# Where the streamed operands of the split matmuls begin in SBUF: 224 bytes behind a multiple of 256

## Chip, cores and metric

The kernel runs on one core of a Trainium2 chip. The metric is the device time of one execution in microseconds; the time before is the median of three runs.

## What is computed

One encoder layer on x of 512 tokens x 1024 features, in float32: a half-step SwiGLU network, a mixer, a second half-step SwiGLU network and a last RMSNorm. In short (the reference, cut):

```
def swiglu(x, w1, w3, w2):
    return (jax.nn.silu(x @ w1) * (x @ w3)) @ w2

def hybrid_mixer(h, w_in, ...):
    proj = h @ w_in                      # A: 24 heads q,k,v; B: 8 query, 2 key/value heads; 2 gates
    o_a = dilated_attention(...)         # 3 groups of 8 heads, joined by their softmax denominators
    o_b = gqa_axial_attention(...)
    gates = jax.nn.sigmoid((pg + b_gate).reshape(B, S, N_BRANCHES, D))
    merged = gates[:, :, 0] * (o_a @ w_branch_a) + gates[:, :, 1] * (o_b @ w_branch_b)
    return merged @ w_out

    x = x + 0.5 * swiglu(rmsnorm(x, ffn1_norm[l]), ...)
    x = x + hybrid_mixer(rmsnorm(x, mix_norm[l]), ...)
    x = x + 0.5 * swiglu(rmsnorm(x, ffn2_norm[l]), ...)
```

The networks are 1024 x 2816 (w1, w3) and 2816 x 1024 (w2).

## The kernel before

Everything is held transposed: 128 features on the partitions, the 512 tokens along the free axis, 4 bytes an element. x is eight tiles of 128 x 512.

**Split matmuls.** A float32 operand is split into H, a rounded copy in the format fp32r (made by ACT, line 217 for weights), and L, the rest (made by DVE, line 218). `mm3` (lines 230 to 234) then makes one product of three matmuls: weights H by streamed H (line 232), the same weights H by streamed L (233), weights L by streamed H (234). Each of the three is a load of 128 x 128 weights and a stream of 256 or 512 columns. The load for a matmul runs beside the stream of the one before it.

**Weight tiles.** All weights come in tiles of 128 x 1024 from HBM, in the fixed order of `self.order`. `prep` (lines 201 to 220) splits the next one as soon as a buffer of the rings is free. The split goes to the ring `wh` (three pairs of buffers in the pool `wb`), and every fourth tile (number 3 modulo 4 in the order), where the stage has a pool `wx`, goes to `whx`, one pair more. A tile serves 24 matmuls of 512 columns: eight blocks of 128 x 128, three matmuls each. In a Strassen step it also serves 24, of 256 columns.

**Strassen.** Part of the networks' first products (`strassen`, `right`) and most of the projection of q and k are done in Strassen's form with seven instead of eight steps for two feature blocks. The steps A11, A12, S3 and S4 stream halves of h, the normed input (`hH`, `hL`); S1, A22 and S2 stream sums of such halves: `TH`, `TL` in the networks, `TQH`, `TQL` in the projection, where S3 takes its operand from there too. The first network does nine pairs of feature blocks in stretches of 2, 4 and 3, the projection five pairs, the second network ten in stretches of 3, 4 and 3. Between the stretches of a network come the products with w2 that stream `gg`, the activated products (line 446 writes them).

**The other products.** In the mixer `feat` streams h by 512 columns; `token` streams weights against h, for v and for branch B's projections; the branch and output products stream `oH`, `qH` and `mH` (with their L parts); branch B's attention streams `kH` and the flipped probabilities `PTH`.

PE's instructions are in an order written out by hand. The other engines take theirs from the order of the program.

**Where tiles begin.** A pool is laid out when it is opened, tags in the order in which they first appear, each buffer at a multiple of 32 bytes. Pools on the left grow upwards: the constants, then `wb`, then `tmp`, then those of the stage. Pools on the right (`side="right"`) grow downwards: h at the very top, then `bt` with `rel_bias`, then the pool of T. All streamed tiles have sizes that are multiples of 256, so what is behind a pool keeps its start modulo 256 unless a small tile comes between. From the order and the sizes follows where each begins, modulo 256:

| tile | begins at |
|---|---|
| hH, hL | 224 |
| TH, TL in the first network (below `rel_bias` of 96 bytes) | 128 |
| TH, TL in the second network | 224 |
| TQH, TQL; gg; qH, qL, kH, kL, vH, vL; oH, oL; mH, mL; PTH, PTL | 32 |
| weights in the ring wh | 160 |
| weights in the ring whx | 32 |

In the program the small tiles are these: `ms` (line 384) has 16 bytes in each of four buffers, so 32 bytes apart; `nm` and `lq` in branch B's attention (lines 963 and 966) 4 bytes in each of four; `F` (line 824) 64 bytes in each of two.

Of the kernel before, what the change touches and what calls it, by code (L numbers as in the profile page):

```python
# [11 lines left out]
F32 = mybir.dt.float32  # L12
# [41 lines left out]
def tile_at(li):  # L54
    if li < 4:
        return 256 * li, (256 if li < 3 else 128), (0 if li < 3 else 64)
    return GP + 256 * (li - 4), 256, 256
# [8 lines left out]
def f32(t):  # L66
    return t.bitcast(F32)


class Layer:  # L70
    def __init__(self, ctx, tc, a):
        self.tc, self.nc, self.a = tc, tc.nc, a
        ctx.enter_context(tc.manual_schedule(engines={mybir.EngineType.PE}))
        pool = lambda n, **k: ctx.enter_context(tc.tile_pool(name=n, **k))
        self.dram = pool("dram", bufs=1, space=DRAM)
        self.cst = pool("cst", bufs=1)
        self.wb = pool("wb", bufs=1)
        self.tmp = pool("tmp", bufs=4)
        self.psm = pool("psm", bufs=4, space=PSUM)
        self.psa = pool("psa", bufs=4, space=PSUM)  # L80
        nc = self.nc
        c = self.cst
        self.x = [c.tile([128, T], F32, name=f"x{d}") for d in range(NK)]
        self.par = c.tile([128, 48], F32, name="par")
        nc.scalar.dma_start(self.par, a["par"])
        self.ident = c.tile([128, 128], F32, name="ident")
        self.ones = c.tile([128, 1], F32, name="ones")
        nc.vector.memset(self.ones, 1.0)
        self.mhalf = c.tile([128, 4], F32, name="mhalf")
        nc.vector.memset(self.mhalf, -0.5)  # L90
        nc.scalar.activation(self.ones, self.ones, AF.Copy)
        self.r = c.tile([128, 8], F32, name="r")
        self.R = c.tile([128, T], F32, name="R")
        nc.gpsimd.memset(self.R, 0.0)
        self.acc = c.tile([128, T], F32, name="acc")
        self.open_h()
        self.gate_d = self.dram.tile([16, 128, T], F32, name="gate_d")
        self.qk_d = self.dram.tile([2 * NSQ, 128, T], F32, name="qk_d")
        self.items = ([("v", 0), ("v", 1), ("sw", 0), ("v", 2)] + [("g", j) for j in range(2)]
                      + [("qk", f) for f in range(NSQ, 12)] + [("g", j) for j in range(2, 9)]  # L100
                      + [("b", g) for g in range(3)] + [("g", j) for j in range(9, 16)])
        span = {"v": ("wav", 4), "qk": ("waq", 2), "g": ("wg", 1), "b": ("wb", 4)}
        self.order = self.ffn_order("a")
        for kind, n in self.items:
            if kind == "sw":
                self.order += [("swq", at) for at in self.slots(range(0, NSQ, 2))]
                continue
            name, m = span[kind]
            self.order += [(name, m * n + i) for i in range(m)]
        self.order += [("wab", i) for i in range(12)] + [("wo", i) for i in range(8)]  # L110
        self.order += self.ffn_order("b")
        self.raws, self.tiles, self.used, self.wx, self.TQ = {}, [], 0, None, None
        self.cap = len(self.order)
        self.rings = {k: [] for k in BUFS}
        self.index = {it[:2]: n for n, it in enumerate(self.order)}
        self.kind = [self.home(it) for it in self.order]
        self.todo = sorted((n for n, t in enumerate(self.kind) if t != "ws"), key=self.turn_of)
# [263 lines left out]
    def rpow(self, dst, src, inv):  # L381
        nc = self.nc
        n = dst.shape[-1]
        ms = self.tmp.tile([128, 4], F32, tag="ms", name="ms")[:, :n]
        nc.vector.tensor_scalar(ms, src, inv, EPS, op0=ALU.mult, op1=ALU.add)
        nc.gpsimd.tensor_tensor(dst, ms, self.mhalf[:, :n], op=ALU.pow)

# [194 lines left out]

    def bias_open(self, bp):
        self.bp = bp
        self.rel = bp.tile([32, 24], F32, name="rel_bias")
        self.nc.sync.dma_start(self.rel, self.a["rel_bias"])
        self.zd = self.dram.tile([8, 128, NV], F32, name="zd")
        self.vd = self.dram.tile([8, NV], F32, name="vd")
# [163 lines left out]
    def scores_a(self, hp, res):  # L752
        nc, ap, qk = self.nc, self.ap, self.qk[hp]
# [11 lines left out]
        for pair in range(4):  # L765
            banks = [self.aux("S") for _ in range(2)]
            heads = []
            for h in range(2):
                hs, ps, mv = slice(64 * h, 64 * h + 64), banks[h], []
                for u in range(2):  # L770
                    li = 2 * pair + u
                    n, o = tile_at(li)[1], 256 * u
# [13 lines left out]
            for h in range(2):  # L786
                for u in range(2):
                    li = 2 * pair + u
                    off, n, w0 = tile_at(li)
# [4 lines left out]
            for h in range(2):  # L794
                for li in (2 * pair, 2 * pair + 1):
                    off, n, _ = tile_at(li)
# [24 lines left out]
        nc.vector.tensor_mul(L, E, SO[:, :, :, 2:4])  # L821
        nc.vector.tensor_add(MN, L[:, 0], L[:, 1])
        nc.vector.reciprocal(MN, MN)
        F = ap.tile([128, 8, 2], F32, tag="F", name="F", bufs=2)
        nc.vector.tensor_mul(F, E[:, 0], MN)
        res += [P, F]

    def values_a(self, hp, P, F):
        nc, ap, V = self.nc, self.ap, self.V
# [8 lines left out]
        def scale(stage):  # L838
            for h in range(2):
                for li in (2 * stage, 2 * stage + 1):  # L840
                    off, n, _ = tile_at(li)
                    sl = P[h][:, off:off + n]
                    nc.vector.tensor_scalar(sl, sl, F[:, li, h:h + 1], None, op0=ALU.mult)

# [109 lines left out]
    def attn_b(self, pp):  # L954
        nc = self.nc
        qH, qL, kH, kL, vH, vL = self.qH, self.qL, self.kH, self.kL, self.vH, self.vL
        P, po, pend = {}, {}, []

        def score(h, i):
            ps = self.aux("Sb")  # L960
            s = slice(128 * i, 128 * i + 128)
            self.mm3(ps, qH[:, h, s], qL[:, h, s], kH[:, h // 4, :], kL[:, h // 4, :], True, True)
            nm = pp.tile([128, 1], F32, tag="nm", name="nm", bufs=4)
            nc.vector.tensor_reduce(nm, ps, axis=mybir.AxisListType.X, op=ALU.max, negate=True)
            p = pp.tile([128, T], F32, tag="P", name="Pb", bufs=8 + LAG)
            lq = pp.tile([128, 1], F32, tag="lq", name="lq", bufs=4)
            nc.scalar.activation(p, ps, AF.Exp, bias=nm, scale=1.0, accum_out=lq)
            nc.vector.reciprocal(lq, lq)
            nc.vector.tensor_scalar(p, p, lq, None, op0=ALU.mult)
            P[h, i] = p  # L970

        def flip(h, k):
            pt = self.aux("Tb")
            for j in range(4):
                nc.tensor.transpose(pt[:, 128 * j:128 * j + 128], P[h, j][:, 128 * k:128 * k + 128], self.ident)  # L975
            H, L = self.split(pp, pt, [128, T], "PTH", "PTL")
            fs = slice(128 * (h // 4), 128 * (h // 4) + 128)
            pend.append((h, k, vH[:, k, fs], vL[:, k, fs], H, L, k == 0, k == 3))

        def value():  # L980
            h, k, *args = pend.pop(0)
            if k == 0:
                po[h] = self.bank()
            self.mm3(po[h], *args)
            if k == 3:
                nc.scalar.copy(qH[:, h, :], po[h])
                nc.vector.tensor_sub(qL[:, h, :], po[h], f32(qH)[:, h, :])

        for s in range(37 + LAG):
            if s < 32:  # L990
                score(s // 4, s % 4)
            t = s - 4 - LAG
            if 0 <= t < 32:
                flip(t // 4, t % 4)
            if pend and t > 0:
                value()
            yield GAP_B
        assert not pend
# [226 lines left out]
```

## Time and profile before

| | us |
|---|---|
| median of three runs (1282.14 to 1282.67) | 1282.46 |
| the profiled execution | 1282.78 |
| its span, first to last instruction | 1281.0 |
| PE busy | 1266.8 |
| DVE busy | 887.8 |
| ACT busy | 586.5 |
| POOL busy | 118.9 |

PE is busy in 99% of the span, at a mean granted clock of 0.998. The busy time of a matmul is longer than its share of the span, because matmuls overlap: a row gives 394 ns for one of 512 columns, while the next one starts some 230 ns after it. So durations of PE are taken here from stretches of known content and not from the mean of one instruction.

### The profile page before, as it was taken

How to read it: one execution, taken by the hardware profiler on the slowest of the kernel's cores; microseconds unless marked ns; L12 is line 12 of the kernel's file. 1: busy time of each engine (PE TensorE's matmuls, PEld its weight loads, DVE VectorE, ACT ScalarE, POOL GpSimd, SP SyncE). 2: the span in 40 equal slices, each digit the busy share in tenths (PEclk: the TensorE clock that was granted, in tenths of full speed). 3: DMA queues.
4: the chain of work that ended last, by engine and by line, in shares of the span. 5: the costliest groups of instructions: out<-in, count | busy, mean ns of one | idle time of the engine just before them, and what ended most of it. 6: DMA issues, size and time to landing. Idle time of an engine off the chain costs nothing.

```text
span 1281.0 us, 19956 instructions
## 1 busy us (share of the span) xinstructions
PE 1266.8 (99%) x8002; PEld 1122.1 (88%) x8002; DVE 887.8 (69%) x1339; ACT 586.5 (46%) x867; POOL 118.9 (9%) x124
## 2 busy tenths in 40 slices
PE   9999999999999999999999999999999999999997
PEld 7897999899889999877888878888889989988996
DVE  7784688467783885667557898655577747874775
ACT  8551355145463442635334465543465415532553
POOL 1111101000210212100001100000301000100001
PEclk9999999999999999999999999999999999999999
DMA  8865766241484846632232210345737636743222
GB/s 298 227 187 167 182 190 189 89 109 55 144 218 142 218 131 208 189 116 85 92 111 83 99 66 25 108 163 165 237 89 181 191 90 176 196 148 104 62 83 67
DMA packets 85549, 181.91 MB, mean 142 GB/s; under 512 B 12480, under 2 KB 19024, under 8 KB 85456
## 3 DMA queue, kind: packets, MB, share of 16 engines
q1 hardware_dynamic: 67904, 140.74, 32.6%
q0 software_dynamic: 16832, 39.34, 15.2%
q8 instruction: 63, 1.03, 0.3%
q10 hardware_dynamic: 720, 0.55, 0.1%
q14 instruction: 30, 0.25, 0.1%
HBM read 168.98 MB, written 15.29 MB: 144 GB/s over the span
## 4 chain that ended last, share of the span: by engine, by line
PE 93%; DVE 3%; issue 1%; DMA 1%; ACT 1%; POOL 0%; SPq 0%; POOLq 0%; DVEq 0%
PE mm L232 24%; PE mm L234 24%; PE mm L233 24%; PE Y L232 3%; PE Y L234 3%; PE Y L233 3%; PE X L232 2%; PE X L234 2%; PE X L233 2%; PE S L785 1%; PE mm L836 1%; PE Tb L975 1%; PE T L854 1%; PE Sb L233 0%; PE Sb L234 0%
## 5 line engine op out<-in xcount | busy, mean ns | idle before, releaser
L217 ACT CAST wh<-wr 128x1024 fp32r<-128x1024 f32 x142 | 148.8, 1049 | 224.8 <-PE mm L233 142.0
L218 DVE TENSOR_TENSOR wl<-wr,wh 128x1024 fp32r<-128x1024 f32 x142 | 173.3, 1221 | 56.9 <-ACT wh L217 56.2
L232 PE MATMUL mm<-hH,wh 128*128 128x256 f32 (+1 forms) x600 | 200.5, 334 | 0.4 <-ACT hH L368 0.3
L234 PE MATMUL mm<-hH,wl 128*128 128x256 f32 (+1 forms) x600 | 196.3, 327 | 1.0 <-DVE wl L218 1.0
L233 PE MATMUL mm<-hL,wh 128*128 128x256 f32 (+1 forms) x600 | 196.1, 327 | 0.3 <-DVE hL L369 0.3
L232 PE MATMUL mm<-gg,wh 128*128 128x512 f32 (+1 forms) x376 | 143.1, 380 | 0.0
L234 PE MATMUL mm<-gg,wl 128*128 128x512 f32 (+1 forms) x376 | 142.6, 379 | 0.0
L233 PE MATMUL mm<-gg,wh 128*128 128x512 f32 (+1 forms) x376 | 142.5, 379 | 0.0
L232 PEld LDWEIGHTS mm<-hH,wh 128*128 128x128 f32 x600 | 112.9, 188 | 14.8 <-issue 3.2
L234 PEld LDWEIGHTS mm<-hH,wl 128*128 128x128 f32 x600 | 112.7, 188 | 12.4 <-DVE wl L218 1.4
L233 PEld LDWEIGHTS mm<-hL,wh 128*128 128x128 f32 x600 | 112.8, 188 | 10.1 <-DVE hL L369 0.8
L217 ACT CAST wh<-wa 128x1024 fp32r<-128x1024 f32 x48 | 50.4, 1050 | 102.5 <-PE mm L233 49.6
L500 DVE TENSOR_TENSOR u<-mm,R 128x512 f32<-128x512 f32 (+1 forms) x52 | 33.8, 649 | 85.0 <-PE mm L234 84.7
L218 DVE TENSOR_TENSOR wl<-wt,wh 128x1024 fp32r<-128x1024 f32 x48 | 58.7, 1223 | 38.1 <-ACT wh L217 37.6
L234 PE MATMUL mm<-TH,wl 128*128 128x256 f32 x304 | 84.7, 279 | 0.0
L232 PE MATMUL mm<-TH,wh 128*128 128x256 f32 x304 | 84.6, 278 | 0.0
L233 PE MATMUL mm<-TL,wh 128*128 128x256 f32 x304 | 84.6, 278 | 0.0
L232 PEld LDWEIGHTS mm<-gg,wh 128*128 128x128 f32 x376 | 70.8, 188 | 15.3 <-PE mm L234 0.9
L234 PEld LDWEIGHTS mm<-gg,wl 128*128 128x128 f32 x376 | 70.8, 188 | 14.1
L233 PEld LDWEIGHTS mm<-gg,wh 128*128 128x128 f32 x376 | 70.9, 188 | 13.8
L217 ACT CAST wh<-ws 128x1024 fp32r<-128x1024 f32 x48 | 50.4, 1051 | 71.0 <-PE mm L233 52.3
L218 DVE TENSOR_TENSOR wl<-wa,wh 128x1024 fp32r<-128x1024 f32 x48 | 58.6, 1221 | 31.2 <-ACT wh L217 31.0
(233 smaller groups left out, 3171.3 us busy)
## 6 DMA issues: line engine op xcount, KB each, us to landing
wr<-in_w2a SPq DMA_DIRECT2D x22, 512.0 KB, 3.3
wr<-in_w2b SPq DMA_DIRECT2D x22, 512.0 KB, 3.5
wt<-in_w13b SPq DMA_DIRECT2D x20, 512.0 KB, 4.1
wa<-in_w13b SPq DMA_DIRECT2D x20, 512.0 KB, 3.5
wt<-in_w13b POOLq DMA_DIRECT2D x20, 512.0 KB, 6.1
wt<-in_w13a SPq DMA_DIRECT2D x18, 512.0 KB, 3.5
wt<-in_w13a POOLq DMA_DIRECT2D x18, 512.0 KB, 6.2
wa<-in_w13a SPq DMA_DIRECT2D x18, 512.0 KB, 3.4
```

Source lines behind the costliest of these rows:

```text
L217: self.nc.scalar.copy(H, raw)
L218: self.nc.vector.tensor_sub(L, raw, f32(H))
L232: mm(out, lH, rH, start=start, stop=False, skip_group_check=more)
L233: mm(out, lH, rL, start=False, stop=False, skip_group_check=more)
L234: mm(out, lL, rH, start=False, stop=stop, skip_group_check=more)
L500: nc.vector.tensor_mul(u, ps, R)
L785: nc.tensor.matmul(*args, start=True, stop=True)
L836: nc.tensor.matmul(oc, v, p, start=st, stop=sp)
L854: nc.tensor.transpose(ps[:, 128 * b:128 * b + 128], P[h][:, c0 + 128 * b:c0 + 128 * b + 128], self.ident)
L975: nc.tensor.transpose(pt[:, 128 * j:128 * j + 128], P[h, j][:, 128 * k:128 * k + 128], self.ident)
```

## The change

Tiles move, and nothing else. A tile `even` of 64 bytes that nothing uses becomes the first in the pool `tmp`. `ms` grows to 64 bytes a buffer, `nm` and `lq` too, `F` to 128 and `rel_bias` to 256; each is cut back to its old shape where it is used. So all behind `tmp` on the left moves up by 64 + 4 x 32 = 192 bytes, and its start of 32 becomes 224; the ring whx is among it. `PT` and the probabilities move by 128 more (160 becomes 224), the flipped probabilities by 256 more. On the right T of the first network moves from 128 to 224. h stays at 224, and the ring wh, which lies below `tmp`, at 160.

```diff
+        self.tmp.tile([128, 16], F32, tag="even", name="even", bufs=1)
...
-        ms = self.tmp.tile([128, 4], F32, tag="ms", name="ms")[:, :n]
+        ms = self.tmp.tile([128, 16], F32, tag="ms", name="ms")[:, :n]
...
-        self.rel = bp.tile([32, 24], F32, name="rel_bias")
+        self.rel = bp.tile([32, 64], F32, name="rel_bias")[:, :24]
...
-        F = ap.tile([128, 8, 2], F32, tag="F", name="F", bufs=2)
+        F = ap.tile([128, 16, 2], F32, tag="F", name="F", bufs=2)[:, :8]
...
-            nm = pp.tile([128, 1], F32, tag="nm", name="nm", bufs=4)
+            nm = pp.tile([128, 16], F32, tag="nm", name="nm", bufs=4)[:, :1]
...
-            lq = pp.tile([128, 1], F32, tag="lq", name="lq", bufs=4)
+            lq = pp.tile([128, 16], F32, tag="lq", name="lq", bufs=4)[:, :1]
```

## Rows read from the trace of the kernel before

**Rows 1.** The page: busy us, share, instructions by engine; the chain's shares.

```profile
PE 1266.8 (99%) x8002; PEld 1122.1 (88%) x8002; DVE 887.8 (69%) x1339; ACT 586.5 (46%) x867; POOL 118.9 (9%) x124
...
PE 93%; DVE 3%; issue 1%; DMA 1%; ACT 1%; POOL 0%; SPq 0%; POOLq 0%; DVEq 0%
```

**Rows 2.** Busy time by stretch, PE alone: the seven Strassen stretches.

```profile
core 0: us, PE busy (x), PEclk, DMA share, GB/s
53.44:92.58 39.14, 39.14 (x337) 1.00 0.68 176
139.36:218.12 78.76, 78.76 (x673) 1.00 0.72 187
262.54:321.69 59.15, 59.15 (x506) 1.00 0.29 84
402.08:501.48 99.40, 99.40 (x842) 1.00 0.60 175
954.99:1012.86 57.87, 57.87 (x505) 1.00 0.71 185
1057.28:1133.65 76.37, 76.37 (x674) 1.00 0.72 189
1178.07:1235.39 57.32, 57.32 (x505) 1.00 0.29 86
```

**Rows 3.** The same view: second network; steps on whx begin at 963.47, 974.78, 1062.93.

```profile
954.99:974.78 19.79, 19.79 (x169) 1.00 0.76 176
963.47:966.30 2.83, 2.83 (x26) 1.00 0.66 216
974.78:1012.86 38.08, 38.08 (x338) 1.00 0.69 190
1060.10:1062.93 2.83, 2.83 (x27) 1.00 0.51 185
1062.93:1133.65 70.72, 70.72 (x627) 1.00 0.74 193
```

**Rows 4.** The first network: T at 142.19 (whx), 145.07, 156.28; the others h.

```profile
142.19:145.07 2.88, 2.88 (x27) 1.00 0.56 190
145.07:147.91 2.84, 2.84 (x27) 1.00 0.55 185
153.56:156.28 2.72, 2.72 (x27) 1.00 1.03 162
156.28:159.11 2.83, 2.83 (x26) 1.00 1.07 164
```

**Rows 5.** The projection (TQ, TQ on whx, h) and the last g products.

```profile
404.91:407.76 2.85, 2.85 (x26) 1.00 0.88 295
407.76:410.63 2.87, 2.87 (x26) 1.00 0.72 210
410.63:413.45 2.82, 2.82 (x26) 1.00 1.07 213
1252.03:1257.73 5.70, 5.70 (x49) 1.00 0.00 0
1257.73:1260.61 2.88, 2.88 (x27) 1.00 0.00 0
```

**Rows 6.** Groups by line: casts of raw weight tiles, wr at 160, wt at 32.

```profile
L217 ACT CAST wh<-wr 128x1024 fp32r<-128x1024 f32 x142 | 148.8, 1049 | 224.8 <-PE mm L233 142.0 <-PE mm L234 32.2 <-issue 23.1
...
L217 ACT CAST wh<-wt 128x1024 fp32r<-128x1024 f32 x48 | 50.4, 1049 | 64.5 <-PE mm L233 38.8 <-PE Y L233 15.3 <-issue 6.1
```

**Rows 7.** Stretches of 512 columns: h; oH, qH, mH; g on whx; g.

```profile
36.96:53.44 16.48, 16.48 (x74) 1.00 0.92 247
820.10:931.64 111.54, 111.54 (x482) 1.00 0.61 191
1024.01:1029.46 5.45, 5.45 (x26) 1.00 0.25 90
1029.46:1046.20 16.74, 16.74 (x73) 1.00 0.30 96
```

## The prediction

> **What bounds the kernel now.** I read the busy times and the chain that ended last first [rows 1]. PE is busy for 1266.8 of 1281.0 us and carries 93% of the chain; DVE has 3% and DMA 1%. So the time is what PE's matmuls take one after another, and the rest runs beside them. The chain doesn't say why a matmul takes as long as it does. Their busy times do not help either, since they overlap; what counts is the distance from one start to the next. For that I took, in the view of busy time by stretch, stretches that begin and end with a weight tile. A weight tile of a Strassen step serves 24 matmuls of 256 columns, a tile of the other products 24 matmuls of 512. (The view counts a few matmuls too many, those that straddle an edge; I divide by the count from the code.) The granted clock is 1.00, the level of 2.4 GHz, in each of these stretches, so it explains no difference. Below, "start" is a tile's first byte modulo 256.
>
> The seven Strassen stretches stand in [rows 2]: 63 steps in the first feed-forward network, 177.05 us together, 35 in the projection of q and k, 99.40 us, and 70 in the second network, 191.56 us. That is 2.81, 2.84 and 2.74 us for the same 24 matmuls. At 256 cycles of 2.4 GHz a matmul they would take 2.56 us. The second network, where T begins at 224 like h, is the fastest.
>
> Single steps show that there are three lengths, and little between them [rows 3 to 5]:
> - 2.72 us (113.3 ns a matmul). Only steps whose streamed operand begins at 224 have it.
> - 2.83 us (117.8 ns). Steps with the same streamed operand at 224 have this too; 2.84 with T at 128, 2.85 with TQ at 32, both with weights at 160.
> - 2.88 us (119.8 ns). Steps where streamed operand and weights both begin at 32 (TQ, and the last g products), and T at 128 with weights at 32.
>
> Whether a step with streamed start 224 takes 2.72 or 2.83 us depends on what came before it [rows 3]. The second network begins at 2.83 us and stays there for seven steps. Then comes a step with a tile of the whx ring (weights at 32), and it and the 13 steps behind it, most with weights at 160, take 38.08 us, 2.72 each. After the g products a step takes 2.83 again (1060.10), the first whx step turns it, and that and 25 more take 70.72 us, 2.72 each. A whx step doesn't always turn it: the first one, at 963.47, took 2.83. In the first network a whx step with h turns it as well (153.56), and the next step with T at 128 undoes it (156.28) [rows 4]. In none of the seven stretches does a step with weights at 160 turn 2.83 into 2.72 by itself.
>
> **The change part by part.** No instruction is added or removed but the allocation of a tile that nothing writes or reads. Shapes stay, so ms, nm, lq, F and rel_bias are written and read as before, only at other bytes. Does a start matter to ACT, DVE or the loads? A cast of a weight tile at 160 takes 1049 ns and of one at 32 takes 1049 [rows 6]. I cost the shift on these engines at nothing; DVE is busy 69% of the span and ACT 46% [rows 1], so some tens of ns more on an instruction would stay beside PE. No wait is added. What is left is the streaming on PE.
>
> *Products of 512 columns, weights at 160.* With h at 224 three blocks took 16.48 us, 5.49 a block; the branch and output products, with their operands at 32, took 111.54 us for 20 blocks, 5.58, and two g blocks 16.74, 5.58 as well [rows 7]. The change puts these operands at 224. There are 30 g blocks with weights at 160 and these 20: 50 x 0.085 = 4.3 us less. The last g products, of 256 columns with weights at 160, go from 2.85 a block (5.70 for two) [rows 5] to 2.83: four blocks, 0.1 us less.
>
> *Products of 512 columns on the whx ring.* Eleven g blocks have weights and operand both at 32, and the first of a pair of g blocks takes 5.45 [rows 7]. They will both be at 224. No row shows 224 with 224. The bounds are 5.45, the shortest block of 512 columns, and 5.58: 0 to +1.4 us over eleven blocks. I take 0, since equal starts stay equal starts.
>
> *Strassen steps with weights at 160.* The operand is at 224 everywhere. Bounds 2.72 and 2.83, and which of them holds is the question of what turns a step. Today only the whx tiles at 32 turn it, and the change takes these away: they move to 224.
>
> *Strassen steps on the whx ring*: 15, 9 and 17 of the 63, 35 and 70. Operand and weights both at 224, which no row shows. The bounds are 2.72 (rows with the streamed start 224; no row of 24 such matmuls is shorter) and 2.88 (rows with equal starts). I take 2.88. The reason is that what is read at the same time are two streams, the operand of one matmul and the weights of the next, so their distance should matter and not one start alone: h at 224 gives 2.72 with weights 64 away as with weights 192 away, equal starts give 2.87 and 2.88 in two different products (TQ, and g) [rows 5]. The row nearest in that sense is the one with equal starts.
>
> And behind such a step? Steps of TQ at equal starts are followed by steps of h with weights at 160 that take 2.82 (410.63) [rows 5], never 2.72. So I let all steps with weights at 160 take 2.827, and those on whx 2.875.
>
> The sum by stretch, today's from [rows 2]: first network (11 x 2.827 + 3 x 2.875) = 39.72 for 39.14, (21, 7) 79.49 for 78.76, (16, 5) 59.61 for 59.15: +1.77. Projection (26, 9): 99.38 for 99.40: 0. Second network (16, 5) 59.61 for 57.87, (21, 7) 79.49 for 76.37, (16, 5) 59.61 for 57.32: +7.15. Together +8.9 us. Four stretches will follow g products at 224, and their steps ahead of the first whx step (1, 1, 2 and 2) may begin at 2.72: up to 6 x 0.107 = 0.6 us less, which I count in full, because the products ahead of them will have the very start that they have.
>
> Total: +8.9 - 0.6 - 4.3 - 0.1 = +3.9 us. The profiled execution took 1282.78 us around its span of 1281.0; the median shown is 1282.46. From the median: **1286.3 us**, 0.3% slower. The change speeds up nearly everything that streamed from 32 or 128, and pays by losing the tiles that put the second network into its fast lane.
>
> The Trainium skill speaks against any effect at all. In "TensorE: Matmul & The Clock Gate" (Step-by-step: what each phase is for) it gives PE two independent read ports, so that loading the next weights takes nothing from the running matmul; by it no start matters and the time stays at 1282.5. The steps of 2.72, 2.83 and 2.88 us at one clock do not agree with that [rows 3, 5].
>
> **The rivals.**
> - *The streamed start alone counts (the other side).* Then whx steps at 224 turn the lane as those at 32 did, and every stretch becomes like the second network's: 191.56 / 70 = 2.737 us a step. First network 63 x 2.737 = 172.4 for 177.05, projection 95.8 for 99.40, second network unchanged, and the same 4.4 us on the other products: -4.6 - 3.6 - 4.4 = -12.6, **1269.9 us**. For it: T at 128 and T at 224 differ with the same weights [rows 3, 4]. Against it: the turn comes from a change of the weights' start alone. It decides from about one step in five on: a step in the fast lane is 0.107 us shorter, so 36 of the 168 pay off the 3.9 us of the forecast.
> - *The equal starts cost nothing but turn nothing either.* All 168 steps at 2.827: 178.1, 98.9 and 197.9, so +1.05 - 0.45 + 6.3 = +6.9, less 0.6 and 4.4: +1.9, **1284.3 us**.
> - *Starts don't matter*, and the lanes come from something else, such as the order of products: **1282.5 us**. Against it: 5.58 and 5.49 us a block in long uniform stretches.
>
> **How the numbers follow.** Forecast 0.62, streamed start alone 0.15, equal starts free 0.13, no effect 0.10. The forecast's own bounds are the whx blocks (0 to +1.4), the six steps behind g products, should they be slow after all (+0.6), and some fifteen others in the fast lane (-1.6), so 1284.7 to 1288.3. The range takes in the two cases between and leaves out the fast one: 1282.0 to 1288.5. About 0.2%, 2.6 us, is what a measurement of this kernel can tell from no change. Slower by more (above 1285.0): most of the forecast's 0.62 and a little of the third case, 0.55. Within: the rest of the forecast, most of the third case and the fourth, 0.29. Faster: 0.16.
>
> **What would show it.** Right: in the profile after, steps on whx tiles at 2.87 to 2.88 us in all three parts, other steps at 2.83 behind them, no long run of 2.72; g, branch and output blocks with weights at 160 at 5.49; the second network's stretches at about 59.6, 79.5 and 59.6 us; casts and subtractions as they were. Wrong: stretches of 2.72 behind a whx step (first rival), whx steps at 2.83 (second), or blocks of 5.58 that stay (third). A wait of PE that is not there now would fit none of these cases, since PE's idle time is nearly nothing today.

## The result, and the profile after

| | before | after |
|---|---|---|
| median, us | 1282.51 | 1274.93 |
| the profiled execution, us | 1282.78 | 1274.42 |
| its span, us | 1281.0 | 1272.6 |

The ratio is 0.994, with a 95% interval of 0.9925 to 0.9955: 7.6 us less. The forecast was 1286.3, with a range from 1282.0 to 1288.5. It was wrong in size and in sign.

The page of the changed kernel: busy time by engine, then casts of those raw weight tiles that the change moves, wt, now at 224 (the rows that answer to [rows 1, 6]).

```profile
PE 1259.8 (99%) x8002; PEld 1119.1 (88%) x8002; DVE 888.7 (70%) x1339; ACT 587.2 (46%) x867; POOL 118.7 (9%) x124
...
L218 ACT CAST wh<-wt 128x1024 fp32r<-128x1024 f32 x48 | 50.4, 1050 | 63.4 <-PE mm L234 38.1 <-PE Y L234 15.3 <-issue 4.7
```

The other engines are as they were to within 1 us, and a cast of wt takes 1050 ns where it took 1049. PE has the same 8002 matmuls and 7.0 us less of busy time, of 8.4 us between the two spans. So, as the prediction assumed, nearly all of it is the pace of PE's matmuls. In the rows that follow the columns are those of [rows 2]: the stretch, its length, PE's busy time and instructions, granted clock, DMA share, GB/s. First the seven Strassen stretches after, which answer to [rows 2]:

```profile
52.90:92.11 39.21, 39.21 (x338) 1.00 0.69 175
138.41:215.78 77.37, 77.37 (x673) 1.00 0.73 190
259.64:317.66 58.02, 58.02 (x506) 1.00 0.28 85
397.68:494.53 96.85, 96.85 (x842) 1.00 0.64 180
945.46:1004.01 58.55, 58.55 (x506) 1.00 0.72 186
1047.87:1125.35 77.48, 77.48 (x674) 1.00 0.72 186
1169.21:1227.33 58.12, 58.12 (x506) 1.00 0.30 86
```

By part they are 174.60 us in the first network, 96.85 in the projection, 194.15 in the second network: 465.60 together, where the kernel before needs 177.05 + 99.40 + 191.56 = 468.01. The prediction had 178.8, 99.4 and 198.7, less 0.6.

Then steps in the second network (first stretch, then the first two steps of the second), and in the projection, one at a time or three together. Steps on whx begin at 953.94, 965.30 and 403.33:

```profile
953.94:956.82 2.88, 2.88 (x27) 1.00 0.67 218
956.82:965.30 8.48, 8.48 (x75) 1.00 0.78 163
965.30:968.17 2.87, 2.87 (x27) 1.00 0.90 256
968.17:976.33 8.16, 8.16 (x75) 1.00 0.53 169
1047.87:1053.52 5.65, 5.65 (x50) 1.00 0.49 129
...
403.33:406.21 2.88, 2.88 (x27) 1.00 0.81 226
406.21:414.37 8.16, 8.16 (x75) 1.00 0.76 197
```

A whx step, operand and weights both at 224, takes 2.87 to 2.88 us. Behind the first one three steps take 8.48 us, 2.83 each. Behind the second three take 8.16, 2.72 each, and so does every step with weights at 160 from there to the end of the stretch. In the projection the first whx step, one of TQ, does it. Over the kernel 107 of the 127 steps with weights at 160 take 2.72 us and 20 take 2.82 to 2.83; all 41 whx steps take 2.87 to 2.88. The loads beside them don't set the pace: three short steps take 8.16 us at a DMA share of 0.53 and at one of 0.76.

Last, products of 512 columns, which answer to [rows 7]: the 20 blocks of the branch and output products, a g block on whx, the three g blocks behind it, and two of the last g blocks of 256 columns [rows 5].

```profile
812.24:922.12 109.88, 109.88 (x482) 1.00 0.63 194
1014.99:1020.45 5.46, 5.46 (x25) 1.00 0.23 88
1020.45:1036.93 16.48, 16.48 (x73) 1.00 0.31 98
1243.77:1249.42 5.65, 5.65 (x49) 1.00 0.00 0
```

A block with weights at 160 now takes 5.49 us. So the 8.4 us between the two profiled executions are 2.4 in the Strassen stretches, 1.7 in the 20 blocks (111.54 to 109.88), 30 x 0.087 = 2.6 in the g blocks, and 1.7 elsewhere, of which 0.5 at the start (the first stretch begins at 52.90 for 53.44; in the runs below anywhere between 52.85 and 53.71) and 0.9 between the projection's end and the branch products (318.62 us before, 317.71 after).

### The profile page after: what moved, and what is told of

Same layout as the page of the kernel before. It is cut to its first block, busy times and chain, and to the rows that moved or that the text cites. A ratio compares the mean times of both kernels' runs of the same rounds, so it can differ in the third digit from the quotient of the medians.

```text
span 1272.6 us, 19956 instructions
## 1 busy us (share of the span) xinstructions
PE 1259.8 (99%) x8002; PEld 1119.1 (88%) x8002; DVE 888.7 (70%) x1339; ACT 587.2 (46%) x867; POOL 118.7 (9%) x124
## 4 chain that ended last, share of the span: by engine, by line
PE 91%; DVE 4%; issue 1%; DMA 1%; ACT 1%; POOL 0%; SPq 0%; POOLq 0%; DVEq 0%
PE mm L233 24%; PE mm L235 23%; PE mm L234 23%; PE Y L233 4%; PE Y L235 3%; PE Y L234 3%; PE X L233 2%; PE X L235 2%; PE X L234 2%; PE mm L837 1%; PE Tb L976 1%; PE S L786 1%; PE T L855 1%; DMA d<-SO 1%; DVE wl L219 1%
## 5 line engine op out<-in xcount | busy, mean ns | idle before, releaser
L218 ACT CAST wh<-wa 128x1024 fp32r<-128x1024 f32 x48 | 50.4, 1050 | 101.7 <-PE mm L234 47.3
```

Source lines behind the costliest of these rows:

```text
L218: self.nc.scalar.copy(H, raw)
```

## Experiments

In all of them the same instructions run, and only starts differ. A step is said to turn those behind it when they go from 2.83 to 2.72 us. To move the weights alone, a ring's tiles were made 256 bytes wider and used from a byte further on, so that whatever lies behind keeps its start. "All the rest" of a kernel is its median less its Strassen stretches. For the changed kernel that is 1274.9 - 465.6 = 809.3 us.

**T alone.** The kernel before with one of the moves.

```diff
-        self.rel = bp.tile([32, 24], F32, name="rel_bias")
+        self.rel = bp.tile([32, 64], F32, name="rel_bias")[:, :24]
```

> The kernel before with one of its moves alone: T of the first network goes from 128 to 224; all other operands, and the whx tiles, stay at 32. Theory A (what counts is how far apart the streamed operand and the weights begin, and a change of that distance turns the lane): the first network now has the starts of the second network of before, so its 63 steps cost 191.56 / 70 = 2.737 us each, 172.4 us for 177.05: 1282.5 - 4.6 = 1277.9 us, and every block of 512 columns stays as it was. Rival B (the streamed start of 224 alone brings the short steps, whatever the weights do): the same here, so this run sizes the share of T and does not tell A from B. Rival C (the gain comes from the blocks of 512 columns and the projection, T is worth nothing): 1282.5 us, first network 177 us.

Measured: 1278.58 us, ratio 0.9969 (0.9957 to 0.9981). Its three stretches of the first network:

```profile
53.44:92.27 38.83, 38.83 (x338) 1.00 0.69 176
139.08:215.77 76.69, 76.69 (x673) 1.00 0.74 191
260.22:317.88 57.66, 57.66 (x505) 1.00 0.28 85
```

173.18 us for 177.05: 3.9 less, where 4.6 was expected. With its operands in one place the first network does nearly what the second one did (2.75 us a step for 2.74).

**The whx tiles back at 32**, on the changed kernel. In `ring`:

```diff
+        k = 16 if tag == "whx" else 0
-        return tuple(pool.tile([128, 1024], F32R, tag=t, name=t, bufs=bufs) for t in ("wh", "wl"))
+        return tuple(pool.tile([128, 1088], F32R, tag=t, name=t, bufs=bufs)[:, k:k + 1024] for t in ("wh", "wl"))
```

> The changed kernel with the whx tiles back at 32 (the ring's tiles are 256 bytes wider and used from byte 64 on); every streamed operand stays at 224. Theory A (distance): whx steps take 2.72 us for 2.88 and turn the lane as they do in the second network of before, so 41 x 0.155 = 6.4 us less than the changed kernel: 1268.6 us; the eleven g blocks on whx are 64 bytes ahead of the operand, which no row shows, at 5.45 to 5.58: 0 to +1.4. The stretches of all 168 steps together 168 x 2.735 = 459.5 us. Rival B (the streamed start alone): whx steps at 32 and at 224 cost alike, 1274.9 us, whx steps 2.88. Rival D (only tiles at equal starts turn the lane when every operand is at 224): whx steps 2.83 and no turning, 168 x 2.827 = 474.9 us of steps, 1284 us.

Measured: 1270.22 us, ratio 0.9903 (0.9889 to 0.9916). The Strassen stretches sum to 458.68 us, 6.9 less than in the changed kernel, all whx steps at 2.72 but two; theory A had 459.5. But all the rest is 2.2 us longer. The cause stands in stretches of g products like the one that answers to 1012.86:1057.28 of before (44.42 us) and to 1004.01:1047.87 of after (43.86). Below are the whole stretch, its third block (whx), the three behind that (weights at 160), and the Strassen stretch that follows it:

```profile
1000.20:1044.69 44.49, 44.49 (x194) 1.00 0.35 105
1011.19:1016.79 5.60, 5.60 (x25) 1.00 0.26 93
1016.79:1033.59 16.80, 16.80 (x73) 1.00 0.28 94
1044.69:1120.85 76.16, 76.16 (x673) 1.00 0.71 189
```

The g blocks that have 32 against 224 take 5.59 to 5.60 us, more than the 5.45 of equal starts and even above the 5.45 to 5.58 that I had given as bounds. That is half of it. The other half lies in blocks whose own tiles did not move: the three with weights at 160 take 5.60 each, where such blocks of the changed kernel take 5.49 (1020.45). So a block of 512 columns can have two lengths as well, and here a whx tile brings the longer one. The Strassen stretch behind these products takes 2.72 us a step from its first step on, where it begins at 2.83 in the changed kernel.

**All weights at 160**, the operands at 224: `k = 48 if tag == "whx" else 0` in the same place.

> The changed kernel with the whx tiles at 160 as well, so that all weights begin at one place and all streamed operands at another, 64 bytes apart. Theory A (a change of distance turns the lane, constant distance never does): each stretch begins at 2.83 us and stays there, 168 x 2.827 = 474.9 us of steps for about 466 in the changed kernel, and the whx g blocks go from 5.45 to 5.49: 1284 us, no better than the kernel before. Rival B (the streamed start of 224 alone brings the short steps): whx steps 2.72 like the others, 168 x 2.73 = 458.6 us, 1268 us.

Measured: 1285.26 us, ratio 1.002 (1.0011 to 1.0029). The projection, the first stretch of the second network, and the sum of all seven:

```profile
401.87:500.80 98.93, 98.93 (x841) 1.00 0.62 176
951.84:1011.20 59.36, 59.36 (x506) 1.00 0.70 184
...
sum 474.88, PE 474.88; mean PE 67.84
```

All 168 steps take 2.827 us. With every operand at 224 and no weight tile that differs there isn't one step of 2.72. That rules out rival B, the prediction's first rival: it is not the streamed start that brings the short steps. And it is the state that the prediction forecast for the changed kernel, at very nearly its price. This kernel and the changed one differ only in the whx tiles, so by their effect on the steps behind them those tiles, dearer themselves, bring 10 us net.

**A price list.** Each Strassen stretch has a weights' start of its own, the other products go through all eight.

```diff
+        name, key = self.order[n][:2]
+        at = 32 * (n % 8)
+        if name[:2] == "sw":
+            at = 32 * (3 if name[2] == "q" else sum(key[0] >= e for e in GROUPS[name[2]][1:]) + (0 if name[2] == "a" else 4))
+        k = (at - (224 if tag == "whx" else 160)) % 256 // 4
```

> The changed kernel with a weights' start of its own in each Strassen stretch: 0, 32, 64, then 96 in the projection, then 128, 160, 192, on both rings; weight tiles of all other products go through 0, 32, ... 224 by their number modulo 8. Operands stay at 224. A list of prices, not a fast kernel. Theory A (distance): steps of a stretch all have one length, since nothing turns the lane: 2.83 us at 160 and at 32 (64 bytes either way, the lane in which a stretch begins), between 2.72 and 2.88 for the others, and blocks of 512 columns from 5.44 (weights at 224, equal) over 5.49 (160) to 5.58 (32) and others between. Rival B (streamed start alone): all stretches alike at 2.72 or 2.83, all blocks of 512 columns alike at 5.49.

Measured in a single execution: 1288.77 us. The stretches have 14, 28, 21, 35, 21, 28 and 21 steps and weights at 0, 32, 64, 96, 128, 160 and 192. Behind them three blocks of the output product, weights at 160, 192 and 224:

```profile
53.71:93.47 39.76, 39.76 (x337) 1.00 0.68 174
140.41:216.58 76.17, 76.17 (x673) 1.00 0.74 192
261.12:320.26 59.14, 59.14 (x506) 1.00 0.28 83
400.59:500.26 99.67, 99.67 (x841) 1.00 0.62 175
953.46:1013.93 60.47, 60.47 (x505) 1.00 0.68 181
1058.49:1137.64 79.15, 79.15 (x674) 1.00 0.69 182
1182.20:1241.00 58.80, 58.80 (x506) 1.00 0.28 83
...
913.19:918.70 5.51, 5.51 (x26) 1.00 0.64 215
918.70:924.29 5.59, 5.59 (x25) 1.00 0.28 98
924.29:929.74 5.45, 5.45 (x26) 1.00 0.32 96
```

Divided by their steps: 2.84, 2.72, 2.82, 2.85, 2.88, 2.83 and 2.80 us. Equal starts, 2.88, are known from after. So the length does follow the distance between weights and operand, and the pairs of before fall on the same list: T at 128 with weights at 160 is 32 apart (2.84 us, as 0 against 224), TQ at 32 with weights at 160 is 128 apart (2.85, as 96 against 224), T at 128 with weights at 32 is 160 apart (2.88, as 128 against 224) [rows 4, 5]. Of 512 columns only two starts are cheap, 224 (equal, 5.45) and 160 (5.49 to 5.51, though 5.60 behind whx tiles at 32); the others lie at 5.59 to 5.61. One point speaks against theory A as I had put it: the stretch at 32 takes 2.72 from its first step on, though nothing in it changes, while I had expected 2.83.

**Two starts**: the cheapest of the list for each kind, with `k` as above.

```diff
+        at = 32 if self.order[n][0][:2] == "sw" else 224
```

> The changed kernel with a weights' start for each kind of product, on both rings: 32 in the Strassen steps (64 bytes ahead of the operand at 224), 224 (equal) in everything else. Theory A (the distance between weights and operand sets the length): Strassen steps 2.72 us from the first step of a stretch on, as at 32 in the list of starts, 168 x 2.721 = 457.1 us for 465.6 in the changed kernel; blocks of 512 columns 5.45 us (about 80 blocks at 5.49 to 5.60 so far: -5 us or so); products that stream weights against h, both at 224 now, 5.45 for about 5.6 a block: -3 us. Together some 1274.9 - 8.5 - 5 - 3 = 1258.5 us. Rival E (short steps in the list of starts came from the mixed products ahead of that stretch, and uniform products leave PE in the slower lane): Strassen steps 2.83 or more, 474.9 us, so 1276 us.

Measured: 1275.19 us, ratio 0.9943 (0.993 to 0.9957). Projection, and the first stretch of the second network:

```profile
399.47:494.67 95.20, 95.20 (x841) 1.00 0.63 183
943.49:1002.85 59.36, 59.36 (x506) 1.00 0.70 184
```

In the projection 2.72 us a step from the first to the last, in all six stretches of the networks 2.827, with the same operand and weights' starts. So a step whose weights and operand begin 64 bytes apart has two lengths, 2.72 and 2.83, and a stretch without changes keeps the one in which it begins. Rival E was right for the networks. The blocks of 512 columns came as expected (5.44), and all the rest is 1275.2 - 471.2 = 804.0 us, 5.3 less than in the changed kernel.

**All moves but that of T**: the changed kernel with `rel_bias` at 96 bytes again.

> The change without its move of T: T of the first network stays at 128, all else as in the changed kernel. Theory A: T at 128 with weights at 160 is a distance of 32 (2.84 us in the list of starts), with weights at 224 one of 96 (2.82); every such step takes the lane away again, so steps of h stay at 2.83 to 2.88. First network 63 x 2.83 = 178.3 us for 174.6 in the changed kernel: 1274.9 + 3.7 = 1278.6 us. Second network and projection as in the changed kernel. If equal starts on whx turned the lane for the steps of h whatever T does, some 20 of them take 2.72: 1276.5 us.

Measured: 1277.62 us, ratio 0.9961 (0.9947 to 0.9975). The first network takes 39.45 + 78.73 + 58.93 = 177.11 us for 174.60. Steps of its first stretch: h on whx (224 and 224); two of h with weights at 160. Then two of its second stretch, behind another such step on whx: T at 128; h with weights at 160.

```profile
61.77:64.64 2.87, 2.87 (x26) 1.00 0.60 183
64.64:70.08 5.44, 5.44 (x50) 1.00 0.87 188
...
156.09:158.93 2.84, 2.84 (x26) 1.00 0.73 116
158.93:161.65 2.72, 2.72 (x26) 1.00 0.95 269
```

The step at equal starts turns the two steps of h behind it to 2.72. T at 128 takes 2.84, but it doesn't always end the short steps, as it did at 156.28 of before [rows 4]: the step of h behind it at 158.93 takes 2.72. So the last case of the expectation is right in kind (it let some 20 steps of h turn; 16 do). The two halves of the change don't add: T alone is worth 4.0 us, the rest alone 5.2, both together 7.6. In the first network's stretches T's move is worth 3.9 us alone and 2.5 on top of the rest.

**TQ at 32, with its weights moved along.** Each step of the projection has the distance of the changed kernel, but the operand's start changes between 224 (h) and 32 (TQ).

```diff
+        name, key = self.order[n][:2]
+        q = name == "swq" and key[1] in ("S1", "S2", "S3", "A22")
+        at = (32 if q else 224) if tag == "whx" else (224 if q else 160)
+        k = (at - (224 if tag == "whx" else 160)) % 256 // 4
...
+            self.TQ = [tp.tile([128, 4160], F32R, name=f"TQ{c}")[:, 16:4112].rearrange("p (a b n) -> p a b n", a=4, b=4) for c in "HL"]
```

> The changed kernel with TQ, the projection's sums, back at 32, and their weights moved with them: 224 for those on the ring wh (64 bytes behind the operand, as 160 is to 224) and 32 for those on whx (equal). h and its weights as in the changed kernel. So each step of the projection has the distance that it has in the changed kernel, at other places, and the operand's start jumps between 32 and 224 from step to step. Theory A (distance alone): the projection takes 96.9 us as in the changed kernel, 2.72 behind the first whx step, 1274.9 us. Rival F (the start of 224 itself counts, or the jump of the operand's start undoes the lane, as the projection of before suggests): steps of TQ 2.83 or more and h behind them 2.83, projection 98.9 to 99.4, 1277 us.

Measured: 1277.23 us, ratio 0.9958 (0.9946 to 0.9971). The projection; its first whx step (TQ and weights both at 32); the two steps of h behind that; later a whx step of h (224 and 224) with the three steps behind it; and two steps more:

```profile
398.29:497.13 98.84, 98.84 (x841) 1.00 0.61 176
403.95:406.83 2.88, 2.88 (x27) 1.00 0.81 206
406.83:412.48 5.65, 5.65 (x50) 1.00 0.99 257
426.67:429.54 2.87, 2.87 (x26) 1.00 0.97 363
429.54:437.70 8.16, 8.16 (x74) 1.00 0.88 199
463.30:466.02 2.72, 2.72 (x26) 1.00 0.51 193
466.02:468.85 2.83, 2.83 (x27) 1.00 0.11 42
```

98.84 us for 96.85, with the same distances: distance alone is not the whole. Behind the equal step of TQ, h takes 2.83, as in the kernel before [rows 5]; behind the equal step of h, 2.72. The last two rows are a step of TQ behind another equal step of TQ, 2.72, and the h behind that, 2.83. All eight equal steps that have a step behind them go the same way: it takes 2.72 where the operand's start stays (once for h, twice for TQ) and 2.82 to 2.83 where it changes (five times). So it doesn't take the start of 224. Nor does every change of the operand's start end the short steps: the three at 429.54 are one of h and two of TQ.

**Everything at 32.** The changed kernel shifted as a whole by 64 bytes, since the expectation took it as open whether the start of 224 counts.

```diff
-        self.tmp.tile([128, 16], F32, tag="even", name="even", bufs=1)
+        self.tmp.tile([128, 32], F32, tag="even", name="even", bufs=1)
...
+        hp.tile([128, 48], F32, name="odd")
...
+        k = 16 if tag == "wh" else 0
```

> The changed kernel shifted as a whole: h, T, TQ and all other streamed operands begin at 32, the weights of the ring wh at 224 (64 bytes behind, as 160 is to 224), those of whx at 32 (equal). Distances and their changes are those of the changed kernel, and no operand's start jumps. If only the distance counts, as long as the operands all begin at one place: Strassen steps 465.6 us as in the changed kernel, projection 96.9, 1274.9 us. If the start of 224 itself counts, which the run with TQ at 32 left open beside the jump: steps behind whx steps 2.83 and the projection about 98.8, all steps some 20 x 0.107 to 107 x 0.107 longer: 1277 to 1286 us.

Measured: 1275.16 us, ratio 0.9935 (0.9922 to 0.9949). The sum of its seven Strassen stretches:

```profile
sum 465.60, PE 465.60; mean PE 66.51
```

It is that of the changed kernel to the last digit. The start of 224 is nothing in itself. What counts is how far apart weights and operand begin, how the weights' start changes, and whether the operands begin at one place.

**Mixed starts**: 160 and 32 in the Strassen steps, as with whx at 32, and 224 elsewhere.

```diff
+        at = (32 if tag == "whx" else 160) if self.order[n][0][:2] == "sw" else 224
```

> The changed kernel with weights at 160 (ring wh) and 32 (whx) in the Strassen steps, as in the run with whx at 32, and at 224, equal to the operand, in all other products on both rings, as in the run with two starts. Theory (a change of the weights' start between steps turns the lane, whatever lies ahead of the stretch): steps as with whx at 32, 458.7 us, up to 1.5 more if stretches that follow equal starts begin in the slower lane; the rest as with two starts, 1275.2 - 471.2 = 804.0 us: 1263 to 1264.5 us. Rival (products of 512 columns at equal starts leave PE in a lane that such changes don't turn): steps 2.83 throughout, 474.9 us: 1279 us.

Measured: 1262.98 us, ratio 0.985 (0.9836 to 0.9863), Strassen stretches 458.54 us. Stretches that follow equal starts begin at 2.83 and are turned by their first whx step, so the two gains add.

**One change a stretch**: as two starts, but the second step's weights at 160.

```diff
+        sw = [self.order[n - i][0][:2] == "sw" for i in range(3)]
+        at = (160 if sw[1] and not sw[2] else 32) if sw[0] else 224
```

> The run with two starts (all Strassen weights at 32, all others at 224) with one step changed in each of the seven stretches: the second step's weights at 160. So there are two changes of the weights' start a stretch and none behind them. If one change of the weights' start is enough to turn the lane for good, steps from the second or third on take 2.72 in all seven stretches, 168 x 2.722 = 457.5 us, 804.0 + 457.5 = 1261.5 us. If a stretch begins in the slower lane and a single change doesn't turn it, the six stretches of the networks stay at 2.83 as with two starts: 1275 us. In between, about 2.5 us for each stretch of 21 or 28 steps.

Measured: 1262.74 us, ratio 0.9849 (0.9836 to 0.9863). First step of the second network (32), second (160), and the 19 behind them (32):

```profile
937.21:940.03 2.82, 2.82 (x25) 1.00 0.46 167
940.03:942.86 2.83, 2.83 (x27) 1.00 0.44 70
942.86:994.54 51.68, 51.68 (x459) 1.00 0.74 198
```

51.68 / 19 = 2.72. The first stretch of the second network takes 57.33 us for 59.36 with two starts, by one tile moved. It is the same in all six stretches of the networks. A change of the weights' start and back turns the steps, and one is enough in each of these six stretches. This kernel and the one with mixed starts are 12 us faster than the changed kernel and 1.5% faster than the one before.

## Why the prediction was wrong

*What bounds the kernel, and where a change could show* was right: hardly anything but PE's pace moved, and the clock was 1.00 in every stretch shown.

*Blocks of 512 columns* were right: 5.49 us at 160 (-4.3 us forecast; 1.7 + 2.6 = 4.3 measured), 5.46 on whx for 5.45 (0 forecast), 0.05 less for each two of the last g blocks.

*Steps on the whx ring* were right: 2.875 forecast, 2.87 to 2.88 measured. The reason given for that choice, that the distance between operand and weights counts and not one start, is what the price list and the shifted kernel show. One reading in it is off: with the operand at 224, weights at 160 and at 32 are not 64 and 192 bytes away but 64 on either side, modulo 256.

*Steps with weights at 160 behind them* are the step that failed. "So I let all steps with weights at 160 take 2.827": 107 of 127 take 2.720, and 107 x 0.107 = 11.4 us is more than the whole error in the Strassen stretches, 8.9 - 0.6 + 2.4 = 10.7. I held that only tiles at 32 turn a step, and that the change takes them away. In fact a change of the weights' start between steps can turn them, to any of the three starts tried (32, 160 and 224), and the change leaves that in place: the whx tiles go from 128 bytes away from the ring wh to 64 away from it. The run with one change a stretch shows that changing is enough, the run with all weights at 160 that without it nothing turns, and the changed kernel that a tile at equal starts turns as well as one at 32. Why such a change turns steps, no run shows.

The evidence on which I relied was a step of h at 2.82 behind an equal step of TQ [rows 5]. That row differs from what the change makes in two things: starts are equal, and the operand's start jumps from 32 to 224 right behind. I laid it to the first. The run with TQ at 32 brings the same pair of steps back, equal and then 2.83, with distances that turn the steps when nothing jumps, and in it TQ behind an equal step of TQ takes 2.72; the shifted kernel shows that the place 224 has no part in it. In the kernel before no step at equal starts is followed by one with the operand at the same place and weights 64 bytes away. So no row of it could have settled the point, and a chance of 0.62 on one side of it was too much.

*Six steps behind g products at 2.72*, worth 0.6 us, didn't come: 1047.87:1053.52 shows two at 2.83, and the other stretches begin likewise. The operands' start ahead of a stretch doesn't decide how it begins: with the whx tiles back at 32 and the same operands, these four stretches do begin at 2.72. With two starts, the networks' stretches begin in the long steps and the projection's in the short ones.

*The rivals.* "The streamed start alone" (1269.9) had the turning right and its reason wrong: with whx steps at 2.878 for 2.72 it would be 41 x 0.158 = 6.5 us more, 1276.4, near the measured 1274.9. So what happened lay between the forecast and a rival, a cross of the one's whx price and the other's turning, and I had given that cross only "some fifteen" steps of room. "The equal starts turn nothing" (1284.3) fell with the same step as the forecast. "Starts don't matter" is far off: moving nothing but starts gives 1262.7 to 1288.8 us for the same instructions. The sentence of the Trainium skill that I set beside it ("TensorE: Matmul & The Clock Gate", Step-by-step: what each phase is for: loading the next weights takes no read bandwidth from the running matmul) doesn't hold for the pace here, if it is read as there, that no start matters: moving the weights alone, operands untouched, took the kernel from 1274.9 to 1285.3 and to 1262.7 us. Whether it is read bandwidth that is lost, no run shows.

## What to carry to other kernels

Where PE is the bound, weights and streamed operands should be laid out as deliberately as loops are: measure the pace for each distance between their starts, put all streamed operands at one start, and choose the weights' start for each kind of product. When a row is taken as evidence for a new case, list everything in which it differs from that case, and if two things differ, give both readings a case of their own with a price. And where a fast and a slow pace exist for the same instructions, ask what switches between them and whether the change keeps that, not only which tiles do it today.

## What the runs showed that was not expected

- With 256 columns a distance of 64 bytes has two stable paces, 113.3 and 117.8 ns a matmul (2.72 and 2.83 us a step), and PE stays in one for a whole stretch of 35 steps without a change. One step with weights elsewhere, and back, takes it from the slower to the faster one. No stretch of these runs went back to the slower pace while its operands all began at one place.
- Not every change turns it: in the changed kernel the first whx step of the second network (953.94) doesn't, the second (965.30) does. Why not is open. How a stretch begins depends on the weights of the products ahead (behind g products with whx at 32 for 224 it begins at 2.72 for 2.83), but by what rule, and what a jump of the operand's start does beyond the steps shown, is open too.
- Blocks of 512 columns have two lengths as well with weights at 160 and the operand at 224, 5.49 and 5.60 us, and there the whx tiles at 32 that shorten the Strassen steps bring the longer one.
- The cheapest distance differs by length: equal starts are among the dearest for 256 columns (2.88 us a step; 64 bytes 2.72) and the cheapest for 512 (5.44 us a block; others up to 5.61).
- Why the place where a tile begins costs up to 6% of a step (2.88 us for 2.72) was not tested; the runs show only that it is the same when everything is shifted by 64 bytes.
